# A hybrid mixer trunk: new step costs for the planner that interleaves the instruction streams, and mixer steps ordered behind the dense matmuls on TensorE

## The chip, the cores and the metric

The kernel runs on one core of one Trainium2 chip. The metric is the device time of one execution in microseconds (us); of several runs the median is given. Engines are named as the profile names them: PE is TensorE (PEld its weight loads), DVE VectorE, ACT ScalarE, POOL GpSimd, and SP the engine that issues the DMAs here.

## The reference

One layer, 1024 frames of width 1024, float32. The input is normed and projected by one matrix; three groups of heads (mLSTM, retention, RWKV-7) work on the columns of the result; what they give is projected back; a gated feed-forward follows.

```python
h = rmsnorm(x, ln1_g[l])
p = h @ w_in[l]
pm, pr, pw = jnp.split(p, [M_COLS, M_COLS + R_COLS], axis=-1)
ym = mlstm_group(pm, ...)          # 4 heads, chunkwise state
yr = retention_group(pr)           # 6 heads, chunkwise state
yw = rwkv7_group(pw, ...)          # 6 heads, generalised delta rule
x = x + jnp.concatenate([ym, yr, yw], axis=-1) @ w_out[l]
h = rmsnorm(x, ln2_g[l])
x = x + (jax.nn.silu(h @ w_gate[l]) * (h @ w_up[l])) @ w_down[l]
return rmsnorm(x, lnf_g)
```

In RWKV-7 each frame changes a 64x64 state S per head: `S = S * w - (S kk) (kk a)^T + v k^T`. That is the part that can't be done all at once.

## The kernel before

**The work.** Every float32 operand of a large product is split into a high and a low part (`split_hi` on ACT, line 90; `split_lo` on DVE, line 93), and each product is three matmuls: high by high, high by low, low by high. Two kinds of these are called *dense* here:

- the products by columns in `three` (lines 119 to 121): 128 weights columns by 512 frames, 24 matmuls for a tile, given out in four quarters of 6. They make the 15 channel-major tiles of the in-projection for two halves of 512 frames, and the out-projection.
- the products by frames in `tok_proj` (lines 729 to 731): 128 frames by 256 columns (264 in the first group), 24 matmuls for a tile, given out in two halves of 12.

All other matmuls of the first stage belong to the *mixers*: small ones (64 to 512 columns) between which DVE, ACT, POOL and DMAs work.

**RWKV-7.** The 6 heads are 3 pairs, the frames 2 halves of 8 chunks of 64 frames; so there are 6 pieces (pair i, half h). For each piece:

1. `rwkv_prep` / `rwkv_half` begins with two matmuls (lines 385 and 387), and ends its larger part with 16 Gram matmuls (line 460) whose masked results stand in the tile `E`.
2. `rwkv_inverse` inverts 32x32 triangles: blocks of E go by DMA to DRAM (line 497) and come back to all partitions (line 507), DVE runs a loop of 15 rounds (lines 519 and 522), the result goes to DRAM (line 528) and back into E (line 532), DVE transposes it (line 535), and two rounds of small matmuls (lines 540 and 546) finish it.
3. `rwkv_chain_pair` runs 8 chunks one after the other, each in three steps: matmuls at line 581, an ACT copy `pm` (line 583); matmuls at lines 586 and 590, ACT copies into X (lines 592 and 593); matmuls at lines 597 and 600, a DVE update of X (line 607), with which the next chunk begins. There are 48 chunks in all. The preparation of a piece of the next pair waits for the chain of the same half of this pair, and the chain of a piece waits for its inverse.

mLSTM and retention are 8 chunks each of `attention`.

**The order of the work.** All of these, nine in number, are generators. `weave` runs them against a planner's clock: a step `yield cost, delay` moves the clock by its cost on PE, and makes the generator ready again after the delay; `yield "name"` waits for a `signal`. Of the ready generators the first in the list goes on: the chain, the inverse, the preparation, the output of RWKV, the norms, the attention, and then the three that hold the dense work (`sharing`). So the numbers in the yields decide between which dense matmuls each mixer step is written down. They are worth nothing on the chip itself; there only the order counts. The framework's compile-time scheduler takes the order in which the kernel is written down as the priority, and may still move an instruction ahead of others of its engine where it thinks these are not ready. On the chip PE takes its matmuls in the compiled order.

After the weave come the out-projection of the second half of frames (with the splits of the first operands of the feed-forward beside it) and the feed-forward (lines 1200 to 1202 and 1385 to 1387). The change does not touch these.

Of the kernel before, what the change touches and what calls it, by code (L numbers as in the profile page):

```python
# [23 lines left out]
KT = 8  # L24
# [30 lines left out]
def trunk_kernel(ctx: ExitStack, tc: tile.TileContext, a: dict, out: bass.AP):  # L55
    nc = tc.nc
    V, S, G, PE, SY = nc.vector, nc.scalar, nc.gpsimd, nc.tensor, nc.sync
# [58 lines left out]
    def three(ps, w, xh, xl, ks=range(KT)):  # L116
        for k in ks:
            hi, lo = w[k]
            PE.matmul(ps, lhsT=hi, rhs=xh[:, k, :], start=(k == 0), stop=False)  # L119
            PE.matmul(ps, lhsT=hi, rhs=xl[:, k, :], start=False, stop=False)  # L120
            PE.matmul(ps, lhsT=lo, rhs=xh[:, k, :], start=False, stop=(k == KT - 1))  # L121

    clock, events = [0.0], {}

# [3 lines left out]
    def weave(gens, sharing):  # L131
        live = [[0.0, None, g] for g in gens + sharing]
        holder = None
        while live:
            ready = [math.inf if (holder and s is not holder and s[2] in sharing) else
                     max(s[0], events.get(s[1], math.inf)) if s[1] else s[0] for s in live]
            clock[0] = max(clock[0], min(ready))
            s = next(s for s, r in zip(live, ready) if r <= clock[0])
            got = next(s[2], None)
            if s is holder:  # L140
                holder = None
            if got is None:
                live.remove(s)
            elif isinstance(got, str):
                s[0], s[1] = clock[0], got
            else:
                clock[0] += got[0]
                s[0], s[1] = clock[0] + got[1], None
                if len(got) == 3:
                    holder = s  # L150

    QUARTERS = (range(0, 2), range(2, 4), range(4, 6), range(6, 8))
    PART = 6 * 0.214

# [34 lines left out]
    NT = 9  # L189
    LAT = 0.93  # L190
    CHAIN, INV, ATT, NORM, MIX = 3.51, 20.16, 3.09, 3.26, 1.28

# [14 lines left out]
    xh, xl = zip(*([act.tile([P, KT, HF], F32R, name="act", tag="act") for _ in two] for _ in two))  # L207
# [86 lines left out]
    w = first[2][0]  # L294
# [86 lines left out]
    def rwkv_half(i, h, r, k, v):  # L381
# [17 lines left out]
        G.tensor_tensor(rn, rn, neghalf[:, 0:8], ALU.pow)  # L399
        yield 0.9, 3.0  # L400

# [29 lines left out]
        if h:  # L431
            signal(f"taken{i}", 3.0)
        yield 2.6, 5.0
        pe = misc_tile()
        for t in range(4):
            for q in range(2):
                PE.matmul(pe[rows_of(q), t * P:(t + 1) * P],
                          lhsT=rn[:, 2 * t + q:2 * t + q + 1].broadcast_to([P, 64]), rhs=ident,
                          start=True, stop=True)
# [8 lines left out]
        for q in range(2):  # L448
# [4 lines left out]
            G.tensor_tensor(E[rows, :, q, 192:256], c3(r)[rows], er[rows, :, 1:65], ALU.mult)  # L453
        yield 0.9, 5.5
        for c0 in range(0, 8, 4):
# [18 lines left out]
        signal(f"ab{i}{h}", 3.0)  # L474
        yield 3.4, 3.0
        V.tensor_tensor(kb, kb, er[:, :, 64:65].unsqueeze(3).broadcast_to([P, 8, 2, 64]), ALU.mult)
# [7 lines left out]
        signal(f"prep{i}{h}", 1.0)  # L484
        yield 0.9, 1.0

# [13 lines left out]
    def rwkv_inverse():  # L500
        for i in range(3):
            for h in range(2):
# [5 lines left out]
                for g in range(4):  # L508
                    S.copy(out=R[lane(g)], in_=MN[lane(g), g::4, :])
                yield 0.0, 8.0  # L510

# [4 lines left out]
                for u in range(1, 31, 2):  # L516
                    n, w = (u + 4) // 4, 31 - u
# [12 lines left out]
                for q in range(2):  # L530
                    for b in range(2):
                        SY.dma_start(out=E[blk(q, b), :, q, col(b)], in_=r_d[b, q].rearrange("c s t -> s c t"))
                yield 0.0, 7.5
                for q in range(2):
# [15 lines left out]
                signal(f"inv{i}{h}", 2.5)  # L550
                yield 0.9, 3.0

# [4 lines left out]
    def rwkv_chain_pair(i):  # L557
        st = None
        for h in range(2):
# [3 lines left out]
            for c in range(8):  # L563
# [19 lines left out]
                S.copy(out=pm, in_=chn[:, 0:64])  # L583
                yield 0.2, LAT
                for q in range(2):
# [7 lines left out]
                S.copy(out=X[64:128, c, 1, :], in_=chn[64:128, 64:128])  # L593
                yield 0.2, LAT
                for q in range(2):
# [19 lines left out]
                if c % 4 == 3:  # L615
                    norm_factor(yw, var, 4, 64e-5)
                    signal(f"yw{len(yws)}", 8.0)
                    yws.append(yw)
                yield 0.4, CHAIN
            signal(f"chain{i}{h}", 1.0)  # L620
# [3 lines left out]
    def rwkv_out():  # L624


        yield "gate"
        for i in range(3):
            for h in range(2):
                yield f"prep{i}{h}"  # L630
                for b in range(2):
                    n = 4 * i + 2 * h + b
                    sl = slice(b * 256, b * 256 + 256)
                    gate = lambda: sb.tile([P, 256], F32, name="gate", tag="gate", bufs=2)
                    add, ga = gate(), gate()
                    SY.dma_start(out=add, in_=add_dram[h][i][:, sl])
                    SY.dma_start(out=ga, in_=gate_dram[h][3 + i][:, sl])
                    G.tensor_tensor(add, add, ga, ALU.mult)
                    gl = gate()
                    SY.dma_start(out=gl, in_=gate_dram[h][i][:, sl])  # L640
                    yield f"yw{n}"
                    if i == 2:
                        yield f"proj{h}"
                    yw = yws[n]
                    pt = misc_tile()[:, 0:256]
                    for c in range(4):
                        for q in range(2):
                            o = rows_of(1 - q)
                            PE.matmul(pt[rows_of(q), c * 64:(c + 1) * 64], lhsT=yw[o, c, :], rhs=ident[o, o], start=True, stop=True)
                    signal(f"out{n}", 0.5)  # L650
                    V.tensor_tensor(gl, gl, pt, ALU.mult)
                    V.tensor_tensor(gl, gl, add, ALU.add)
                    if i < 2:
                        SY.dma_start(out=yw_dram[h][i][:, sl], in_=gl)
                    else:
                        yh, yl = yT[h]
                        split_hi(yh[:, 7, sl], gl)
                        split_lo(yl[:, 7, sl], gl, yh[:, 7, sl])
                    yield 0.9, 0.0

# [46 lines left out]
    def tok_proj(g, ts=range(KT)):  # L707
# [16 lines left out]
        for t in ts:  # L724
# [3 lines left out]
            for k in range(KT):  # L728
                PE.matmul(o, lhsT=xh[h][:, k, sl], rhs=w[k][0], start=(k == 0), stop=False)  # L729
                PE.matmul(o, lhsT=xh[h][:, k, sl], rhs=w[k][1], start=False, stop=False)  # L730
                PE.matmul(o, lhsT=xl[h][:, k, sl], rhs=w[k][0], start=False, stop=(k == KT - 1))  # L731
                if k == 3:
                    yield 12 * 0.42e-3 * n, 0.0, True
            vt = etmp(256, "vt")
# [25 lines left out]
            SY.dma_start(out=v_dram[h][sl, 256 * g:256 * g + 256], in_=vt)  # L760
            cost = 12 * 0.42e-3 * n
            yield (cost, 0.0, True) if t < ts.stop - 1 else (cost, 0.0)
# [335 lines left out]
    def attention():  # L1098
        mlstm = ("mlstm", 2.6, mlstm_load, mlstm_chunk, mlstm_finish, None)
        ret = ("ret", 4.0, ret_load, ret_chunk, ret_finish, ret_store)  # L1100
        for (name, cost, load, chunk, finish, store), start, ts in (
# [437 lines left out]
```

## Time and profile before

| | before |
|---|---|
| median of 3 runs | 1536.41 us (1533.66 to 1537.58) |
| the profiled execution | 1537.23 us, of which the profile's span is 1535.4 us |
| PE busy, share of the span | 1425.2 us, 93% |
| DVE / ACT / POOL busy | 883.0 / 556.7 / 453.3 us |
| first matmul of the feed-forward (line 1200) | at 807.0 us |
| DMA | 165.59 MB, mean 108 GB/s |

The profile shows one execution. PE's busy time counts a matmul from its start until its end, and neighbours overlap; so a busy PE is not a PE at its peak, and what a matmul costs is read from the distance between starts. A wait is put down to the instruction that came last before it ended. "PEclk" is the clock granted to TensorE, as a share of full speed.

### The profile page before, as it was taken

The numbers are of one execution on the slowest core, as the hardware profiler recorded it, in microseconds if no ns is written. First come the engines' busy times: TensorE is split into PE (matmuls) and PEld (weight loads), VectorE is DVE, ScalarE is ACT, GpSimd is POOL, SyncE is SP. The second block draws the span as 40 slices with busy tenths as digits, with TensorE's granted clock in tenths as the row PEclk, the third lists the DMA queues.
The fourth block names the chain that finished last, engine by engine and source line by source line (L and its number), as shares of the span: only waits on it lengthen the run. The fifth ranks groups of instructions, "written<-read, shape, count | busy, mean of one in ns | idle before, by whom it ended". The sixth has DMA issues, their size and how long they took to land. (4 is left out here: it accounts for less than half of the span.)

```text
span 1535.4 us, 23068 instructions
## 1 busy us (share of the span) xinstructions
PE 1425.2 (93%) x8434; PEld 1154.8 (75%) x8434; DVE 883.0 (58%) x1750; ACT 556.7 (36%) x1201; POOL 453.3 (30%) x550
## 2 busy tenths in 40 slices
PE   7988899799997998999997999999999998999996
PEld 5767577787677877887785777777777776887886
DVE  7457567458856767545566544555554555337344
ACT  6343244333332143244554333333332344324222
POOL 3211013234434323324336443444444420000000
PEclk9998799899988999799999999999999999999999
DMA  5132121333421343453632222212222248336333
GB/s 210 50 128 71 40 80 68 86 96 104 122 78 52 95 149 109 123 159 121 218 125 68 76 82 83 74 66 80 83 76 77 75 171 283 98 93 226 109 94 117
DMA packets 122334, 165.59 MB, mean 108 GB/s; under 512 B 37837, under 2 KB 70509, under 8 KB 120941
## 3 DMA queue, kind: packets, MB, share of 16 engines
q1 hardware_dynamic: 122220, 164.13, 33.5%
q8 instruction: 66, 1.08, 0.3%
q14 instruction: 48, 0.39, 0.1%
HBM read 125.27 MB, written 38.81 MB: 107 GB/s over the span
## 5 line engine op out<-in xcount | busy, mean ns | idle before, releaser
L93 DVE TENSOR_TENSOR wlo<-wraw,whi 128x512 fp32r<-128x512 f32 (+1 forms) x210 | 147.0, 705 | 131.0 <-ACT whi L90 130.0
L90 ACT ACTIVATE whi<-wraw 128x512 fp32r<-128x512 f32 (+1 forms) x210 | 127.7, 612 | 209.1 <-PE chain L1386 119.8
L93 DVE TENSOR_TENSOR wlo<-rg,whi 128x512 fp32r<-128x512 f32 x128 | 97.9, 767 | 136.2 <-ACT whi L90 136.1
L729 PE MATMUL acc<-whi,act 128*128 128x256 f32 (+1 forms) x512 | 160.8, 317 | 5.9 <-ACT whi L90 4.8
L730 PE MATMUL acc<-wlo,act 128*128 128x256 f32 (+1 forms) x512 | 154.7, 304 | 3.7 <-DVE wlo L93 3.5
L119 PE MATMUL acc<-act,whi 128*128 128x512 f32 x352 | 151.0, 429 | 6.8 <-ACT whi L90 6.1
L1200 PE MATMUL acc<-act,whi 128*128 128x512 f32 x352 | 141.1, 401 | 15.1 <-ACT work L1303 10.7
L731 PE MATMUL acc<-whi,act 128*128 128x256 f32 (+1 forms) x512 | 152.4, 299 | 0.0
L1385 PE MATMUL chain<-act,whi 128*128 128x512 f32 (+1 forms) x374 | 142.9, 382 | 3.9 <-ACT act L90 3.9
L120 PE MATMUL acc<-act,whi 128*128 128x512 f32 x352 | 144.5, 411 | 1.8 <-DVE act L252 1.8
L121 PE MATMUL acc<-act,wlo 128*128 128x512 f32 x352 | 144.9, 412 | 1.1 <-DVE wlo L93 1.1
L90 ACT ACTIVATE whi<-rg 128x512 fp32r<-128x512 f32 x128 | 79.1, 628 | 178.5 <-PE acc L1201 81.1
L1386 PE MATMUL chain<-act,whi 128*128 128x512 f32 (+1 forms) x374 | 143.0, 383 | 0.8 <-DVE act L93 0.8
L1387 PE MATMUL chain<-act,wlo 128*128 128x512 f32 (+1 forms) x374 | 142.7, 382 | 0.0
L1202 PE MATMUL acc<-act,wlo 128*128 128x512 f32 x352 | 139.3, 396 | 0.2 <-DVE wlo L93 0.2
L1201 PE MATMUL acc<-act,whi 128*128 128x512 f32 x352 | 139.1, 395 | 0.0
L729 PEld LDWEIGHTS acc<-whi,act 128*128 128x128 f32 x512 | 103.8, 204 | 13.6 <-ACT whi L90 5.3
L730 PEld LDWEIGHTS acc<-wlo,act 128*128 128x128 f32 x512 | 104.4, 204 | 8.1 <-DVE wlo L93 5.6
L1200 PE MATMUL misc<-act,whi 128*128 128x512 f32 x264 | 104.6, 396 | 4.7 <-ACT whi L90 4.7
L731 PEld LDWEIGHTS acc<-whi,act 128*128 128x128 f32 x512 | 104.5, 204 | 1.1 <-issue 0.2
L1201 PE MATMUL misc<-act,whi 128*128 128x512 f32 x264 | 104.6, 396 | 0.0
L1202 PE MATMUL misc<-act,wlo 128*128 128x512 f32 x264 | 104.2, 395 | 0.0
(323 smaller groups left out, 2832.3 us busy)
## 6 DMA issues: line engine op xcount, KB each, us to landing
wraw<-in_w_down SPq DMA_DIRECT2D x85, 256.0 KB, 2.7
rg<-in_w_gate SPq DMA_DIRECT2D x22, 512.0 KB, 5.6
rg<-in_w_up SPq DMA_DIRECT2D x22, 512.0 KB, 5.0
a_dram<-work SPq DMA_DIRECT2D x43, 256.0 KB, 2.2
wraw<-in_w_tm SPq DMA_DIRECT2D x40, 256.0 KB, 3.0
rg<-a_dram SPq DMA_DIRECT2D x10, 1024.0 KB, 6.3
v_dram<-vt SPq DMA_DIRECT2D x64, 128.0 KB, 1.9
wraw<-in_w_out SPq DMA_DIRECT2D x32, 256.0 KB, 3.4
```

What stands on the lines that cost most here:

```text
L90: S.activation(hi, src, AF.Copy, scale=scale)
L93: (eng or V).tensor_tensor(lo, src, hi.bitcast(F32), ALU.subtract)
L119: PE.matmul(ps, lhsT=hi, rhs=xh[:, k, :], start=(k == 0), stop=False)
L120: PE.matmul(ps, lhsT=hi, rhs=xl[:, k, :], start=False, stop=False)
L121: PE.matmul(ps, lhsT=lo, rhs=xh[:, k, :], start=False, stop=(k == KT - 1))
L729: PE.matmul(o, lhsT=xh[h][:, k, sl], rhs=w[k][0], start=(k == 0), stop=False)
L730: PE.matmul(o, lhsT=xh[h][:, k, sl], rhs=w[k][1], start=False, stop=False)
L731: PE.matmul(o, lhsT=xl[h][:, k, sl], rhs=w[k][0], start=False, stop=(k == KT - 1))
L1200: PE.matmul(ps, lhsT=hi, rhs=hi_x[:, k, :], start=(start and k == 0), stop=False, skip_group_check=True)
L1201: PE.matmul(ps, lhsT=hi, rhs=lo_x[:, k, :], start=False, stop=False, skip_group_check=True)
L1202: PE.matmul(ps, lhsT=lo, rhs=hi_x[:, k, :], start=False, stop=(stop and k == 3), skip_group_check=True)
L1386: PE.matmul(ps, lhsT=hi, rhs=lo_a[:, sl], start=False, stop=False)
```

## The change

Three things are done, all in the weave of the first stage:

1. The planner's numbers are others. The dense work costs 7 to 12% more (`PART`, a quarter, 6 * 0.214 to 6 * 0.23; a token half from 12 * 0.42e-3 to 12 * 0.47e-3 for each column). The steps of the mixers cost and delay much more: the chain's three steps go from (0.2, 0.93), (0.2, 0.93), (0.4, 3.51) to (0.4, 1.4), (0.45, 1.9), (0.5, 4.2), the loop of the inverse from 20.16 to 30.0, its trips through DRAM from 8.0 and 7.5 to 11.0 and 9.0, an mLSTM chunk from 2.6 to 4.2, a retention chunk from 4.0 to 5.0. The two costs of the output of RWKV and of one step of the preparation become smaller.
2. The planner's clock begins at 10 and not at 0.
3. Every mixer step is traced within `tc.issue_after(dense[0])`, where `dense[0]` is the last dense matmul written down so far (the third of each k). It gives each PE instruction of the step an ordering edge to that matmul: the compile-time scheduler may no longer put it ahead of that matmul. No semaphore is added, since both run on PE. A dense matmul may still be put ahead of a mixer step, and the other engines' instructions get no edge.

No instruction is added or removed. The lines of the changed kernel below line 122 have numbers that are 2 higher.

```diff
@@ three
-            PE.matmul(ps, lhsT=lo, rhs=xh[:, k, :], start=False, stop=(k == KT - 1))
+            dense[0] = PE.matmul(ps, lhsT=lo, rhs=xh[:, k, :], start=False, stop=(k == KT - 1)).ins
...
-    clock, events = [0.0], {}
+    clock, events = [10.0], {}
+    dense = [None]
@@ weave
-            got = next(s[2], None)
+            with nullcontext() if s[2] in sharing or dense[0] is None else tc.issue_after(dense[0]):
+                got = next(s[2], None)
...
-    PART = 6 * 0.214
+    PART, TOK = 6 * 0.23, 12 * 0.47e-3
...
-    LAT = 0.93
-    CHAIN, INV, ATT, NORM, MIX = 3.51, 20.16, 3.09, 3.26, 1.28
+    LAT, CHAIN, INV, ATT, NORM, MIX = (1.4, 1.9), 4.2, 30.0, 4.0, 4.0, 1.6
@@ tok_proj
-                PE.matmul(o, lhsT=xl[h][:, k, sl], rhs=w[k][0], start=False, stop=(k == KT - 1))
+                dense[0] = PE.matmul(o, lhsT=xl[h][:, k, sl], rhs=w[k][0], start=False, stop=(k == KT - 1)).ins
```

Two places show how this moves the instructions on PE. A name left of the arrow is the tile written, those right of it are read; `acc` is the result of dense work, `whi` and `wlo` are split weights, `act` split activations, `chain` the chain's tile, `misc` that of the other mixers.

The first is PE in the third chunk of the first pair. Before, from the chain's first step (L581) to its second (L586, L590):

```order
L581 MATMUL chain<-X,E 64x64 x2
L119 MATMUL acc<-act,whi 128x512
L120 MATMUL acc<-act,whi 128x512
L121 MATMUL acc<-act,wlo 128x512
L119 MATMUL acc<-act,whi 128x512
L120 MATMUL acc<-act,whi 128x512
L121 MATMUL acc<-act,wlo 128x512
L586 MATMUL chain<-pm,E 64x64 x2
L590 MATMUL chain<-st,E 64x64 x2
```

Now, from the same first step (L583):

```order
L583 MATMUL chain<-X,E 64x64 x2
L119 MATMUL acc<-act,whi 128x512
L120 MATMUL acc<-act,whi 128x512
L121 MATMUL acc<-act,wlo 128x512
L119 MATMUL acc<-act,whi 128x512
L120 MATMUL acc<-act,whi 128x512
L121 MATMUL acc<-act,wlo 128x512
L119 MATMUL acc<-act,whi 128x512
L120 MATMUL acc<-act,whi 128x512
L121 MATMUL acc<-act,wlo 128x512
L119 MATMUL acc<-act,whi 128x512
L120 MATMUL acc<-act,whi 128x512
```

One more dense matmul and then the second step follow: 12 stand between the two steps where 6 stood.

The second is PE ahead of the last of the six inverses, where its first round of small matmuls begins (L540, now L542, reading `tq`). Before, with chunks of the retention (L952 to L975) and frame products of the in-projection (L729 to L731) in front of it:

```order
L952 MATMUL misc<-rT 128x128 x6
L962 MATMUL misc<-RR,rT 128x64 x3
L729 MATMUL acc<-whi,act 128x256
L730 MATMUL acc<-wlo,act 128x256
L966 MATMUL misc<-rv,rsw 128x64 x3
L962 MATMUL misc<-RR,rT 128x64 x3
L731 MATMUL acc<-whi,act 128x256
L729 MATMUL acc<-whi,act 128x256
L975 MATMUL misc<-rv,rk 64x64 x6
L730 MATMUL acc<-wlo,act 128x256
L966 MATMUL misc<-rv,rsw 128x64 x3
L540 MATMUL misc<-tq,E 32x32
```

Now, with the chain (L583 to L602) and products of the out-projection (L119 to L121):

```order
L588 MATMUL chain<-pm,E 64x64 x2
L592 MATMUL chain<-st,E 64x64 x2
L120 MATMUL acc<-act,whi 128x512
L121 MATMUL acc<-act,wlo 128x512
L599 MATMUL chain<-X,E 64x64 x2
L602 MATMUL chain<-X,E 64x64 x2
L998 MATMUL misc<-cst,ry 128x128 x3
L119 MATMUL acc<-act,whi 128x512
L583 MATMUL chain<-X,E 64x64
L120 MATMUL acc<-act,whi 128x512
L121 MATMUL acc<-act,wlo 128x512
L542 MATMUL misc<-tq,E 32x32
```

The whole in-projection stands ahead of this place now; the chain's steps follow each other with one to three dense matmuls between them.

More of the change, by code (lines that the diff above doesn't have):

```diff
@@ L1 @@
 import math
-from contextlib import ExitStack
+from contextlib import ExitStack, nullcontext
 from itertools import chain
@@ L399, in rwkv_half @@
         G.tensor_tensor(rn, rn, neghalf[:, 0:8], ALU.pow)
-        yield 0.9, 3.0
+        yield 2.6, 4.0
         S.activation(t1, th, AF.Identity, scale=hka[:, i:i + 1], bias=oka[:, i:i + 1])
@@ L432, in rwkv_half @@
             signal(f"taken{i}", 3.0)
-        yield 2.6, 5.0
+        yield 2.0, 6.0
         pe = misc_tile()
@@ L453, in rwkv_half @@
             G.tensor_tensor(E[rows, :, q, 192:256], c3(r)[rows], er[rows, :, 1:65], ALU.mult)
-        yield 0.9, 5.5
+        yield 1.2, 7.0
         for c0 in range(0, 8, 4):
@@ L474, in rwkv_half @@
         signal(f"ab{i}{h}", 3.0)
-        yield 3.4, 3.0
+        yield 2.2, 4.0
         V.tensor_tensor(kb, kb, er[:, :, 64:65].unsqueeze(3).broadcast_to([P, 8, 2, 64]), ALU.mult)
@@ L484, in rwkv_half @@
         signal(f"prep{i}{h}", 1.0)
-        yield 0.9, 1.0
+        yield 1.0, 1.0
     blk = lambda q, b: slice((1 - q) * 64 + b * 32, (1 - q) * 64 + b * 32 + 32)
@@ L509, in rwkv_inverse @@
                     S.copy(out=R[lane(g)], in_=MN[lane(g), g::4, :])
-                yield 0.0, 8.0
+                yield 0.0, 11.0
                 mf = MN.rearrange("p s t -> p (s t)")
@@ L532, in rwkv_inverse @@
                         SY.dma_start(out=E[blk(q, b), :, q, col(b)], in_=r_d[b, q].rearrange("c s t -> s c t"))
-                yield 0.0, 7.5
+                yield 0.0, 9.0
                 for q in range(2):
@@ L550, in rwkv_inverse @@
                 signal(f"inv{i}{h}", 2.5)
-                yield 0.9, 3.0
+                yield 1.7, 3.0
     def rwkv_chain():
@@ L583, in rwkv_chain_pair @@
                 S.copy(out=pm, in_=chn[:, 0:64])
-                yield 0.2, LAT
+                yield 0.4, LAT[0]
                 for q in range(2):
@@ L593, in rwkv_chain_pair @@
                 S.copy(out=X[64:128, c, 1, :], in_=chn[64:128, 64:128])
-                yield 0.2, LAT
+                yield 0.45, LAT[1]
                 for q in range(2):
@@ L618, in rwkv_chain_pair @@
                     yws.append(yw)
-                yield 0.4, CHAIN
+                yield 0.5, CHAIN
             signal(f"chain{i}{h}", 1.0)
@@ L658, in rwkv_out @@
                         split_lo(yl[:, 7, sl], gl, yh[:, 7, sl])
-                    yield 0.9, 0.0
+                    yield 0.7, 0.0
     def rwkv_gate():
@@ L730, in tok_proj @@
                 PE.matmul(o, lhsT=xh[h][:, k, sl], rhs=w[k][1], start=False, stop=False)
-                PE.matmul(o, lhsT=xl[h][:, k, sl], rhs=w[k][0], start=False, stop=(k == KT - 1))
+                dense[0] = PE.matmul(o, lhsT=xl[h][:, k, sl], rhs=w[k][0], start=False, stop=(k == KT - 1)).ins
                 if k == 3:
-                    yield 12 * 0.42e-3 * n, 0.0, True
+                    yield TOK * n, 0.0, True
             vt = etmp(256, "vt")
@@ L760, in tok_proj @@
             SY.dma_start(out=v_dram[h][sl, 256 * g:256 * g + 256], in_=vt)
-            cost = 12 * 0.42e-3 * n
+            cost = TOK * n
             yield (cost, 0.0, True) if t < ts.stop - 1 else (cost, 0.0)
@@ L1098, in attention @@
     def attention():
-        mlstm = ("mlstm", 2.6, mlstm_load, mlstm_chunk, mlstm_finish, None)
-        ret = ("ret", 4.0, ret_load, ret_chunk, ret_finish, ret_store)
+        mlstm = ("mlstm", 4.2, mlstm_load, mlstm_chunk, mlstm_finish, None)
+        ret = ("ret", 5.0, ret_load, ret_chunk, ret_finish, ret_store)
         for (name, cost, load, chunk, finish, store), start, ts in (
```

## The prediction

> **What bounds the kernel now.** I read the page first, then the stretches by stage, PE's timeline, PE's waits, and then the stretches around each inverse.
>
> ```profile
> span 1535.4 us, 23068 instructions
> ...
> PEclk9998799899988999799999999999999999999999
> ```
>
> ```profile
> 0.00:171.00 171.00, 143.63 (x788) 111.49 (x788) 101.73 (x206) 75.89 (x140) 34.32 (x60) 0.92 0.33 108
> 171.00:807.00 636.00, 591.80 (x4628) 487.80 (x4628) 409.74 (x1022) 241.13 (x664) 214.78 (x349) 0.93 0.36 109
> 807.00:1535.40 728.40, 689.75 (x3020) 555.55 (x3018) 371.56 (x523) 239.70 (x397) 204.21 (x142) 0.99 0.32 107
> ```
>
> The first row gives the clock granted to PE in 40 slices: the dips lie in the first half. In the stretches the columns are time, then busy time of PE, PEld, DVE, ACT, POOL, then that clock. The feed-forward from 807 us on has PE busy for 690 of 728 us at a clock of 0.99, and the change doesn't touch it. The first 807 us are where PE has gaps (592 of 636 us) and a clock of 0.92 to 0.93. Busy time hides how much is lost there, so I go by the distance between starts:
>
> ```profile
> 184.74 0.34 PE L581 MATMUL chain<-X,E 128*64 128x64 f32 x4
> 185.80 0.39 PE L119 MATMUL acc<-act,whi 128*128 128x512 f32 x1
> 186.03 0.40 PE L120 MATMUL acc<-act,whi 128*128 128x512 f32 x1
> ...
> 193.28 0.34 PE L581 MATMUL chain<-X,E 128*64 128x64 f32 x4
> 318.15 0.28 PE L731 MATMUL acc<-whi,act 128*128 128x256 f32 x1
> 318.27 0.28 PE L729 MATMUL acc<-whi,act 128*128 128x256 f32 x1
> ```
>
> A dense matmul of 512 columns costs 0.23 us, one of 256 costs 0.12 us, at full clock. These are the new planner's numbers (PART is 6 x 0.23; TOK at 256 columns is 12 x 0.12). In this piece nothing is lost: a chunk of the chain takes 193.28 - 184.74 = 8.54 us and holds 30 dense matmuls (6.9 us) and 10 mixer matmuls, which leaves 0.16 us for each mixer matmul. Where it is lost, the waits say:
>
> ```profile
> PE misc L540 <- DVE tq L535: 10.7, 3, 7.5
> PE chain L586 <- ACT pm L583: 7.6, 5, 1.9
> PE chain L597 <- ACT X L593: 6.7, 3, 5.3
> PE misc L460 <- DVE E L468: 4.9, 4, 3.1
> PE acc L729 <- ACT whi L90: 4.8, 2, 4.4
> PE chain L581 <- DVE X L607: 4.7, 1, 4.7
> ```
>
> The inverse and the chain lead: PE comes to a mixer step before its operand is there, and everything behind it in the queue stands. How much that is with the lower clock it brings, I take from the five stretches from the last Gram matmul of a piece (L460) to the first matmul that needs its inverse (L540), pieces 2 to 6:
>
> ```profile
> L460 PE MATMUL misc<-E,kb x32: 272/272/419, 129.8 to 137.3; 64*128 64x128 f32 x32
> L540 PE MATMUL misc<-tq,E x32: 191/191/212, 215.4 to 215.9; 32*32 32x32 f32 x32
> L460 PE MATMUL misc<-E,kb x32: 272/272/373, 272.3 to 277.6; 64*128 64x128 f32 x32
> L540 PE MATMUL misc<-tq,E x32: 191/191/212, 331.7 to 332.2; 32*32 32x32 f32 x32
> L460 PE MATMUL misc<-E,kb x32: 272/272/373, 371.4 to 375.2; 64*128 64x128 f32 x32
> L540 PE MATMUL misc<-tq,E x32: 191/191/212, 428.5 to 431.2; 32*32 32x32 f32 x32
> L460 PE MATMUL misc<-E,kb x32: 272/272/550, 465.7 to 473.9; 64*128 64x128 f32 x32
> L540 PE MATMUL misc<-tq,E x32: 191/236/258, 529.5 to 533.0; 32*32 32x32 f32 x32
> L460 PE MATMUL misc<-E,kb x32: 272/272/373, 573.1 to 577.3; 64*128 64x128 f32 x32
> L540 PE MATMUL misc<-tq,E x32: 236/236/257, 642.2 to 645.9; 32*32 32x32 f32 x32
> ```
>
> In the stretches between those places (the same columns as above):
>
> ```profile
> 137.30:215.40 78.10, 70.59 (x417) 50.85 (x416) 43.85 (x116) 21.78 (x61) 8.83 (x32) 0.83 0.21 55
> 277.60:331.70 54.10, 44.82 (x367) 40.26 (x365) 28.94 (x95) 14.51 (x54) 13.32 (x29) 0.87 0.32 87
> 375.20:428.50 53.30, 49.98 (x371) 36.99 (x369) 43.24 (x143) 20.67 (x63) 22.45 (x48) 1.00 0.41 108
> 473.90:529.50 55.60, 49.67 (x408) 45.20 (x407) 37.25 (x113) 12.13 (x43) 17.90 (x32) 0.88 0.25 72
> 577.30:642.20 64.90, 56.26 (x488) 50.56 (x487) 43.15 (x127) 20.91 (x60) 21.82 (x33) 0.86 0.32 96
> ```
>
> **The inverse windows.** Between those two places the compiled order has, before: 207 dense matmuls of 512 columns and 108 mixer matmuls; 235 of 256 and 71; 108 of 512 and 138; 289 of 256 and 62; 211 of 256 and 155. At 0.23, 0.12 and 0.15 us (a mixer matmul: an estimate, just under the chain's 0.16, since many others are as small) that is PE work of 63.8, 38.9, 45.5, 44.0 and 48.6 us. They took 78.1, 54.1, 53.3, 55.6 and 64.9 us. So 14.3, 15.2, 7.8, 11.6 and 16.3 us were lost, 65 us in all, at a clock of 0.83 to 0.88 in all but the third.
>
> After: 283 of 512 and 86; 275 of 256 and 156; 132 of 512, 97 of 256 and 58; 249 of 256 and 159; 57 of 512 and 154. That is 78.0, 56.4, 50.7, 53.8 and 36.2 us of PE work. The total work is the same, so what counts is what is lost. The shortest inverse took 53.3 us, and the first four windows now hold about that or more; so PE arrives when the result is there. I take 3 us lost in each (bounds: 0, as in the chunk above, and what each lost before), 12 instead of 48.9: **-37 us**. The sixth piece is the reverse: 36.2 us of work for an inverse of 53.3 to 64.9 us. I take 56, near the three shorter ones, since with fewer dense products DVE has fewer evictions in its queue: 20 lost instead of 16.3, **+4 us** (bounds 17 and 29: +1 and +12).
>
> [...]
>
> **The chain.** Of its waits (7.6 + 6.7 + 4.7 = 19 us) I put half inside the windows above. Of the other half I take **-5 us** (bounds 0 and -9.5): between its steps stand 12 dense matmuls instead of 6 early on, which is 2.8 us against 1.4. Late on they stand tighter. In the last ten chunks seven have about 3.3 us of PE work in all three steps. One of the quickest chunks in the trace:
>
> ```profile
> 376.55 0.34 PE L581 MATMUL chain<-X,E 128*64 128x64 f32 x4
> ...
> 377.48 0.33 PE L586 MATMUL chain<-pm,E 64*64 64x64 f32 x4
> ...
> 378.98 0.34 PE L597 MATMUL chain<-X,E 128*64 128x64 f32 x4
> ```
>
> 0.93 and 1.50 us, though some dense work stood between them; the third step, which has a DVE update behind it and not one ACT copy, I estimate at 2 us, a third more than the second. That makes 4.4 us, 1.1 over the work, times seven: **+8 us** (bounds 0, if the waits overlap other mixers' work, and 8.54 - 3.3 = 5.2 a chunk, +37).
>
> **The rest.** The preparations (from L385 to the last L460) hold about as much PE work after as before in the order; I take nothing for them, and nothing for the clock's start at 10, since the order up to the first inverse is the same but for 26 dense matmuls. DMA issues move with their steps, and SP's queue is taken in order too:
>
> ```profile
> SPq L101 <- DVE R L522: 34.7, 10, 17.7
> ```
>
> Weight loads (L101) stood behind the issue of an inverse's result (L528), which waited for its DVE loop, for up to 17.7 us. The loop counts 30 instead of 20 now, so that issue is written down later, behind more weight loads. That can only help dense work; I take nothing, since PE's own waits for weights are the few above. DVE and ACT see the same instructions; more dense work inside a window also means more evictions and splits in front of the inverse's loop, which is the second rival.
>
> **The edge.** A mixer step behind a dense matmul now waits where that matmul waits for its split weights (4.8 us above, once 4.4). I take nothing, since the order puts the step there on purpose and the weights are loaded ahead. [...] Were that wait doubled by it, the sum would be 5 us worse.
>
> Sum: -37 + 4 - 5 + 8 = -30 us. Against the profiled execution of 1537.2 us that is 1507 us; the median of the runs lies 0.8 us lower, so **1506 us**.
>
> **The rivals.**
>
> 1. *All of it goes* (0.20). If the windows lose nothing (first four -49, sixth +1), the chain's waits outside go (-9.5), and the preparations, with the clock no longer halved beside them, give 10 (an estimate from the 0.07 of clock that 171 to 807 us lacks, 45 us if all of it were matmul time, less what the windows hold): -68, 1469 us. For it: where PE is fed, a chunk loses nothing. Against: the waits at L460 are not paced anew.
> 2. *DVE sets the pace* (0.10). The inverse is mostly a DVE loop, and DVE takes its queue in order: 43.2 of 53.3 us and 43.2 of 64.9 us busy in the third and fifth rows. If a window with more dense work has a longer loop for the evictions in it, the first four lose what they lost, and -5 + 4 + 0 to 8 remain: 1536 to 1544, about 1538 us.
> 3. *The cover runs out, slower* (0.13). Dense work is spent early (12 between steps), and the last inverse and the chain behind it stand bare. Its price: -37 - 5, the sixth inverse at 64.9 (+12), seven chunks at 8.54 us (+37): +7, 1544 us. It decides from about 7.5 us for a bare chunk: (37 + 5 - 12) / 7 = 4.3 over 3.3. Against: those 8.54 us contain 6.9 us of dense work that isn't there.
> 4. *The change does not do what it says.* The compiled order excludes that for the numbers. The edge alone may do nothing; the forecast rests on the order, whichever made it.
>
> **How the numbers follow.** The forecast has 0.52 (its own range is 1488 to 1523 us: from 1.5 us lost in a window, the sixth at +1, the chain at -7 and no tail, to 6 us lost in a window, the chain at -2 and the tail at +8), rival 1 0.20, rival 2 0.10, rival 3 0.13; 0.05 lies between. A measurement of this kernel can tell about 0.3%, 4.6 us. Faster: forecast, rival 1 and the 0.05 in between, 0.77. Same: most of rival 2, 0.09. Slower: rival 3 and the rest of rival 2, 0.14. The range takes in rival 1 nearly and rival 2: 1470 to 1540 us.
>
> **What would show it.** Right: the first matmul of the feed-forward at about 777 us instead of 807; the wait at the inverse's matmuls (now L542) concentrated in the sixth piece, 15 to 25 us in one; a granted clock near 1.0 in the stretches of pieces 2 to 5; the chain's early chunks at 12 to 13 us each (48 dense matmuls at 0.23 and 10 others at 0.16 us) and yet no gap on PE. Wrong: a clock still under 0.9 in those stretches, or loops of the inverse that grew with the work beside them (rival 2); chain steps late on over 7 us a chunk (rival 3).

## The result, and the profile after

The change made the kernel slower, by 0.6%: 1543.35 us, the median of 13 runs (1539.38 to 1552.2), beside 1535.65 us, the median of 13 runs of the kernel before on the same chip. The ratio is 1.0059, its 95% interval 1.0039 to 1.0080. Forecast were 1506 us, and 1470 to 1540 us as the range; the time lies outside it. Here and below medians are of all runs, while ratios leave out the few that took over 1.5% longer than the fastest of their kernel (one of the kernel before here, two of chain_first_pair).

The profiled execution took 1540.95 us, 1539.2 us of it span. First the clock granted to PE in 40 slices, then the three stages (time; busy time of PE, PEld, DVE, ACT, POOL; clock), as shown of before:

```profile
PEclk9999998989899989998998999999999999999998
```

```profile
0.00:171.00 171.00, 148.37 (x815) 115.59 (x816) 104.66 (x213) 77.81 (x143) 35.75 (x63) 0.95 0.32 109
171.00:806.40 635.40, 585.07 (x4602) 482.51 (x4602) 397.32 (x1016) 238.45 (x661) 213.04 (x346) 0.92 0.36 109
806.40:1539.20 732.80, 695.99 (x3019) 560.32 (x3017) 369.67 (x524) 240.27 (x398) 205.82 (x142) 0.98 0.32 106
```

The feed-forward, which should have begun at 777 us, begins at 806.4 us, where it began before (807 us), and the clock from 171 us on is 0.92, where it was 0.93. The weave has gained nothing in this execution. How much of the 8 us of the medians lies in it can't be read from one pair of profiles: the runs before_again and after_again, below, show that two executions of one kernel differ by more.

The same five stretches as before, from the last Gram matmul of pieces 2 to 6 (now L462) to the first matmul that needs the piece's inverse (now L542):

```profile
138.70:223.10 84.40, 80.23 (x450) 60.84 (x448) 56.60 (x133) 27.36 (x64) 9.29 (x34) 0.94 0.22 64
308.40:383.80 75.40, 67.26 (x573) 60.04 (x571) 52.02 (x179) 19.35 (x67) 32.32 (x59) 0.90 0.41 108
425.00:484.10 59.10, 52.67 (x340) 42.13 (x339) 39.83 (x116) 14.81 (x43) 19.90 (x34) 0.94 0.29 81
531.20:599.80 68.60, 63.23 (x534) 57.14 (x533) 45.26 (x133) 23.19 (x68) 21.06 (x37) 0.88 0.40 115
648.80:705.40 56.60, 43.37 (x331) 32.98 (x330) 31.53 (x103) 15.32 (x51) 20.62 (x31) 0.89 0.35 102
```

More work does stand in the first four (450 matmuls where there were 417, then 573 for 367, 340 for 371, 534 for 408; the third of these pairs, of the fourth piece, has fewer but larger ones), and together they became longer by just about that work: 46 us for 47.5. To see what each loses, I took from the trace the distance from each matmul's start to the next, and compared it with 0.23 us for a dense matmul of 512 columns, 0.12 us for one of 256, and the median distance of its own line for a mixer matmul. What is over that is lost (us; "again" is a second execution of the same kernel):

| window of piece | before: length, work, lost | before again: lost | after: length, work, lost | after again: lost |
|---|---|---|---|---|
| 2 | 78.1, 57.0, 21.1 | 16.1 | 84.4, 72.0, 12.4 | 13.5 |
| 3 | 54.1, 36.6, 17.5 | 18.3 | 75.4, 56.3, 19.2 | 19.6 |
| 4 | 53.3, 45.0, 8.3 | 8.6 | 59.1, 48.1, 11.0 | 11.9 |
| 5 | 55.6, 41.4, 14.2 | 12.8 | 68.5, 51.1, 17.4 | 16.5 |
| 2 to 5 | 61.1 | 55.8 | 60.0 | 61.5 |
| 6 | 64.9, 44.6, 20.3 | 20.9 | 56.6, 33.8, 22.8 | 23.6 |

Windows 2 to 5 lose 60 us, where 12 were forecast. Only the second loses less than before, in both executions. And hardly any of it is a wait for the inverse. PE's waits over the whole weave, after:

```profile
PE misc L542 <- DVE tq L537: 13.1, 3, 9.6
PE chain L588 <- ACT pm L585: 10.2, 4, 6.4
```

Of the 13.1 us at the inverse's matmul, 9.6 stand ahead of the sixth inverse and the rest at the first (158 to 162 us, inside the second window); in the windows of pieces 3, 4 and 5 PE waits for no inverse at all. In the fourth this is the only wait that the profile gives:

```profile
PE chain L588 <- ACT pm L585: 6.4, 1, 6.4
```

PE at that place, and then ACT:

```profile
437.97 0.34 PE L583 MATMUL chain<-X,E 128*64 128x64 f32 x4
...
439.63 0.28 PE L733 MATMUL acc<-whi,act 128*128 128x256 f32 x1
446.34 0.48 PE L588 MATMUL chain<-pm,E 64*64 64x64 f32 x4 [6.43 <-ACT pm L585]
...
446.96 0.79 PE L119 MATMUL acc<-act,whi 128*128 128x512 f32 x1
447.55 0.63 PE L120 MATMUL acc<-act,whi 128*128 128x512 f32 x1
```

```profile
434.90 0.21 ACT L612 COPY yw<-chain 128x64 f32<-128x64 f32 x1 [2.09 <-DVE X L609]
443.03 1.66 ACT L511 COPY R<-MN 32x256 f32<-32x256 f32 x4 [7.92 <-DMA MN<-ab_d]
444.71 0.22 ACT L613 ACTIVATE ysq<-chain 128x64 f32<-128x64 f32 x1
...
446.10 0.19 ACT L585 COPY pm<-chain 128x64 f32<-128x64 f32 x1
```

The chain's first step was issued at 437.97 us. Its ACT copy `pm` could follow at once, but ACT stands from 435 to 443 us at the inverse's R copies (L511), whose operand MN is still on its way by DMA. `pm` comes at 446.10 us, behind these copies, a statistic and two splits, and PE, with its next dense matmuls queued behind the chain's second step, stands 6.4 us and then runs 512 columns in 0.43 to 0.59 us instead of 0.23, at a granted clock of 0.50 (446.9 to 449.8 us). Over the whole of this execution ACT and DVE start their instructions in the compiled order, line by line (1201 and 1750 instructions; the same in before), and here `pm` comes behind a copy that stood 7.92 us. No planner's number moves the R copies: they are written down right behind the issue of the DMA, ahead of the step's `yield`.

### The profile page after: what moved, and what is told of

The parts are those of the page before. It is cut to its first block, busy times and chain, and to the rows that moved or that the text cites. A ratio compares the mean times of both kernels' runs of the same rounds, so it can differ in the third digit from the quotient of the medians.

```text
span 1539.2 us, 23089 instructions
## 1 busy us (share of the span) xinstructions
PE 1429.4 (93%) x8434; PEld 1158.4 (75%) x8434; DVE 871.6 (57%) x1750; ACT 556.5 (36%) x1201; POOL 454.6 (30%) x550
## 5 line engine op out<-in xcount | busy, mean ns | idle before, releaser
L731 PE MATMUL acc<-whi,act 128*128 128x256 f32 (+1 forms) x512 | 156.6, 308 | 4.6 <-ACT whi L90 3.8
L119 PE MATMUL acc<-act,whi 128*128 128x512 f32 x352 | 149.9, 426 | 6.5 <-ACT whi L90 6.1
L733 PE MATMUL acc<-whi,act 128*128 128x256 f32 (+1 forms) x512 | 151.6, 296 | 0.0
L121 PE MATMUL acc<-act,wlo 128*128 128x512 f32 x352 | 143.9, 409 | 2.1 <-DVE wlo L93 2.1
L731 PEld LDWEIGHTS acc<-whi,act 128*128 128x128 f32 x512 | 101.5, 199 | 11.6 <-ACT whi L90 4.8
L733 PEld LDWEIGHTS acc<-whi,act 128*128 128x128 f32 x512 | 102.5, 200 | 2.5 <-issue 1.7
```

The costliest lines, as they stand in the source:

```text
L733: dense[0] = PE.matmul(o, lhsT=xl[h][:, k, sl], rhs=w[k][0], start=False, stop=(k == KT - 1)).ins
```

## The experiments

Two explanations stood after the profiles: that the windows lose because ACT and DVE stand in their queues for the inverse's transfers (theory Q), whatever the numbers say; and that the new numbers move dense work away from where it is needed (S, later split by part of the table). Rivals were the edge, and the inverse's loop. Ratios are to runs of the kernel before on the same chip; intervals are 95%. "After" and "before" name the kernels on which an edit is made. The letters of the theories are those of the expectations: E the edge, Q the queues that stand at a DMA's landing, D DVE's loop as the pace, S dense work spent too early, O the other numbers as the cost, L the later chain steps.

### numbers_only and edge_only: the two halves of the change

numbers_only is after without the edge:

```diff
-            with nullcontext() if s[2] in sharing or dense[0] is None else tc.issue_after(dense[0]):
-                got = next(s[2], None)
+            got = next(s[2], None)
```

> The new planner numbers without the ordering edge. Theory Q (what PE loses comes from ACT and DVE standing in their queues for DMA landings of the inverse): the edge matters little, within 4 us of the changed kernel (1539 to 1547). Theory E (the edge ate the gain: mixer steps held behind late dense matmuls): 10 to 30 us faster than the changed kernel, 1515 to 1533.

edge_only is before with those lines added, and its old numbers.

> The kernel before with the ordering edge alone. Theory Q: within 4 us of before. Theory E: 5 us or more slower than before.

Measured: 1539.8 us, 1.0033 [1.0005, 1.0061], and 1533.21 us, 0.9987 [0.9968, 1.0006]. The edge by itself can't be told from nothing, and the numbers without it are slower as the whole change is. So the cost lies in the numbers; what the edge does beside them (1.0033 against 1.0059) is within the noise.

### after_r_dma: ACT out of the inverse's transfer

```diff
                 for g in range(4):
-                    S.copy(out=R[lane(g)], in_=MN[lane(g), g::4, :])
+                    SY.dma_start(out=R[lane(g)], in_=ab_d.rearrange("b q c s t -> (b q c) s t")[:, g::4, :])
```

> The changed kernel, but the four ACT copies of R from MN are four DMAs from the same DRAM tile, so ACT no longer stands in its queue until MN has landed. Theory Q: the stalls of PE that end with a chain or attention step just after MN lands (2.6, 3.2, 6.7, 3.0 and 3.6 us in the changed kernel's trace) go, with some of the half-clock time behind them: 12 to 25 us faster than the changed kernel, 1518 to 1531. Theory D (the DVE loop of the inverse sets the length of the windows): no more than 4 us off, 1539 to 1547.

Measured: 1551.12 us, 1.0109 [1.0074, 1.0144], no faster than after (1.0059 [1.0039, 1.0080]), where theory Q had named 12 to 25 us less. Two of PE's waits in the weave:

```profile
PE acc L121 <- DVE wlo L93: 5.6, 2, 5.3
...
PE chain L588 <- ACT pm L585: 3.4, 2, 3.2
```

ACT no longer waits for MN, and PE's wait for `pm` went from 10.2 to 3.4 us as it should. But dense matmuls now wait for `wlo` from DVE, at 445 us 5.3 us in one, close to the place of the 6.4 us of after. DVE there:

```profile
448.37 0.66 DVE L516 TENSOR_TENSOR rt<-MN 128x480 f32<-128x480 f32 x1 [7.66 <-DMA MN<-ab_d]
...
450.67 1.82 DVE L93 TENSOR_TENSOR wlo<-wraw,whi 128x512 fp32r<-128x512 f32 x2
```

DVE too has an instruction in its queue that needs MN, and the evictions and splits behind it wait for 7.7 us. The stall went from one engine's queue to the other's, and MN, whose load is issued 4.8 us later here (438.1 instead of 433.4 us), comes at 448.4 instead of 443.0 us. To take ACT alone out of the way gains nothing; the held kernels below take both.

### after_no_loop: the inverse without its loop

```diff
-                for u in range(1, 31, 2):
+                for u in range(0):
```

> The changed kernel without the 15 rounds of the inverse's DVE loop (the inverse is not computed). Theory D: each inverse is 18 to 33 us shorter, the windows fall to their PE work, some 49 us lost in windows 2 to 5 and 20 in the sixth go: 40 to 65 us faster, 1478 to 1503. Theory Q: the waits at MN stay and only the sixth's wait goes: 8 to 20 us faster, 1523 to 1535.

Measured: 1521.89 us, 0.9921 [0.9899, 0.9942]. Windows 3 and 4, where after has 75.4 and 59.1 us:

```profile
307.60:384.30 76.70, 69.32 (x571) 61.82 (x570) 43.16 (x133) 19.23 (x67) 31.34 (x59) 0.87 0.42 113
422.30:480.80 58.50, 51.92 (x337) 41.46 (x335) 30.83 (x69) 15.80 (x46) 17.88 (x36) 0.94 0.28 82
```

With 9 us of DVE work taken out of each (52.02 and 39.83 against 43.16 and 30.83 us) these windows are as long as in after. The loop doesn't set them. What the kernel gains, some 21 us by the ratios, lies for the most part where PE does wait for the inverse: in the sixth window, which lasts 47.3 instead of 56.6 us, and in the first two (53.0 and 77.1 instead of 58.4 and 84.4 us). The fifth is shorter as well, 62.8 instead of 68.5 us, though PE waits for no inverse there in after; 1.5 us of that is less work between its ends, and the rest isn't explained. Theory D had named 40 to 65 us. By the size of the gain and by windows 3 and 4 it falls, and with it the mechanism of the prediction's second rival.

### chain_numbers and other_numbers: the numbers in two parts

chain_numbers is before with the new numbers of the chain's three steps alone:

```diff
-    CHAIN, INV, ATT, NORM, MIX = 3.51, 20.16, 3.09, 3.26, 1.28
+    LAT, CHAIN, INV, ATT, NORM, MIX = (1.4, 1.9), 4.2, 20.16, 3.09, 3.26, 1.28
...
-                yield 0.2, LAT
+                yield 0.4, LAT[0]
...
-                yield 0.2, LAT
+                yield 0.45, LAT[1]
...
-                yield 0.4, CHAIN
+                yield 0.5, CHAIN
```

> The kernel before with the new numbers of the chain's three steps alone. Theory S (dense work is a fixed amount of cover; slower chain numbers spend it early, and what the chain no longer waits for, attention, the output and the sixth inverse wait for): as slow as the changed kernel or slower, 1540 to 1550. Theory O (it is the other numbers that cost): like before, 1530 to 1539.

other_numbers has all the new numbers but these, and no edge.

> The new numbers without the edge, but with the chain's three steps as before. Theory S: the inverse and the attention get their cover and the chain keeps ahead, 1520 to 1534, faster than before by up to 15 us. Theory O: as slow as the changed kernel, 1540 or more.

Measured: 1576.8 us, 1.0279 [1.0261, 1.0296], and 1518.83 us, 0.9901 [0.9873, 0.9929]. Both go the way of theory S, and further than it said. The change is made of two parts that work against each other: the numbers of the inverse, the attention and the rest gain 15 us, those of the chain cost 43 us by themselves and, on top of the others (1.0033 against 0.9901), about 20. In chain_numbers PE's waits for inverses lead, and one is the longest of the study:

```profile
725.27 0.79 PE L580 MATMUL chain<-X,E 128*64 128x64 f32 x4 [3.17 <-DVE X L606]
746.21 0.31 PE L539 MATMUL misc<-tq,E 32*32 32x32 f32 x2 [20.14 <-DVE tq L534]
```

PE stands for 20 us ahead of the sixth inverse, with 74 us of dense matmuls queued behind that place.

### after_held and before_held: ACT and DVE kept from standing at the transfer

The R copies and DVE's first product on MN are written down 16 of the planner's us after the transfer's issue, where the copies came at once and the product after 11 (or 8, in before), and held by an order edge behind the last ACT copy or split, and the last DVE eviction, split or update of X, that was written down ahead of them (`recent` is set at these):

```diff
-                for g in range(4):
-                    S.copy(out=R[lane(g)], in_=MN[lane(g), g::4, :])
-                yield 0.0, 11.0
+                yield 0.0, 16.0
+                with tc.issue_after(recent["S"]):
+                    for g in range(4):
+                        S.copy(out=R[lane(g)], in_=MN[lane(g), g::4, :])
...
+                with tc.issue_after(recent["V"]):
                     V.tensor_tensor(tv, mf[:, 34:34 + 15 * 66:66].unsqueeze(2).broadcast_to([P, 15, 32]), MN[:, 2:31:2], ALU.mult)
```

> The changed kernel with the inverse's ACT copies and first DVE product written 16 planner us after the load of MN instead of 0 and 11, and held behind the last chain copy, split or eviction written ahead on their engine. Theory Q (ACT and DVE standing in their queues for MN stall PE): the waits of ACT on MN fall from 39 us to under 15, PE's waits on pm copies from 10 us to under 4; 8 to 20 us faster than the changed kernel, 1523 to 1535. Theory S: the waits go elsewhere, and the inverse comes a chunk later: 1540 to 1550.

> The same on the kernel before (16 planner us after the load of MN instead of 0 and 8). Theory Q: 5 to 15 us faster than before, 1520 to 1530. Theory S: 1533 to 1542.

Measured: 1526.9 us, 0.9954 [0.9934, 0.9975], for after, and 1524.31 us, 0.9939 [0.9918, 0.9960], for before: 16 us off the one and 9 off the other. ACT's wait for MN in after's weave, and then in after_held's:

```profile
ACT R L511 <- DMA MN<-ab_d: 39.2, 6, 10.1
```

```profile
ACT R L515 <- DMA MN<-ab_d: 4.1, 2, 3.3
```

At the place of the 6.4 us stall ACT now takes `pm` first, then waits for a weight, and does the R copies without a wait for MN:

```profile
432.19 0.21 ACT L589 COPY pm<-chain 128x64 f32<-128x64 f32 x1 [1.74 <-PE chain L587]
438.47 0.63 ACT L92 ACTIVATE whi<-wraw 128x512 fp32r<-128x512 f32 x1 [6.07 <-DMA wraw<-in_w_cm]
...
439.45 1.66 ACT L515 COPY R<-MN 32x256 f32<-32x256 f32 x4
```

PE's wait for `pm` goes from 10.2 to 2.9 us, and windows 2 to 5 of after_held lose 46.7 us by the same account, where after loses 60.0. The two waits and both times came out as theory Q had said. This part of the loss isn't the change's own: before has it as well (29.1 us of ACT's time at MN, 2.6 in before_held). With the holding, the two kernels can't be told apart (0.9954 and 0.9939), so the 8 us between after and before may lie in such stalls too; that wasn't shown. Nor does a run separate the holding edges from the later place in the order: the edit also moves the rest of the inverse back by 5 (or 8) of the planner's us.

### other_held and other_held_edge: what helps, together

other_held is other_numbers with the same holding; other_held_edge adds the edge.

> The new numbers of all steps but the chain's three, with the R copies and the first VectorE product of each inverse held back behind the last chain work written ahead of them; no edge. Theory Q plus S (the shift of cover and the queues on the inverse's transfer are two separate losses): the gain of the numbers alone (14.5 us) and of the holding (9 to 16 us) add up, 1503 to 1510 us, ScalarE's wait for MN under 8 us in all. Rival O' (both gains come from the same stalls of TensorE, so only one can be had): 1515 to 1520 us. Rival: the holding makes ScalarE late for the gates, no better than the numbers alone or worse, 1519 to 1525 us.

> The kernel of the run other_held with the edge of the change added. Theory E0 (the edge changes nothing, since the scheduler already places the mixers' instructions behind that matmul): within 4 us of other_held. Rival E (the edge keeps ScalarE and VectorE from taking up mixer work early): 5 us or more away from it, in either direction.

Measured: 1506.43 us, 0.9814 [0.9779, 0.9850], and 1499.44 us, 0.9776 [0.9737, 0.9816]. The gains of the numbers and of the holding add up (0.9901 times 0.9939 is 0.984). Between the two kernels lie 7 us, more than the 4 expected, but their intervals overlap: whether the edge helps here stays open. Both are faster than before, by about 2%, and so than after.

### before_again and after_again: how far two executions differ

No edit.

> The kernel before, unchanged, to see how far two profiled executions of one kernel differ. Expected: the first FFN matmul within 3 us of 807.2 us, and 726 to 733 us from there to the end of the span. If the FFN's start lies over 5 us away, differences of some us between profiles say nothing.

> The changed kernel, unchanged, for the same purpose. Expected: the first FFN matmul within 3 us of 806.4 us, and 726 to 733 us from there to the end; windows from the last Gram matmul to the first inverse matmul within 1 us of 58.4, 84.4, 75.4, 59.1, 68.5 and 56.6 us. If the FFN's start comes at 809 or later, the slower time of the change lies in the weave; if at 806, in what differs from run to run behind it.

The stage up to the feed-forward, of before_again and of after_again:

```profile
0.00:794.80 794.80, 721.39 (x5417) 590.44 (x5418) 509.75 (x1228) 316.74 (x805) 249.33 (x409) 0.94 0.36 111
```

```profile
0.00:820.30 820.30, 741.27 (x5416) 605.76 (x5417) 502.65 (x1228) 316.38 (x804) 248.42 (x409) 0.92 0.35 107
```

The feed-forward begins at 794.8 us instead of 807.2, and at 820.3 instead of 806.4. I had expected both within 3 us. So a difference of some 10 us between two profiles of this kernel says nothing, and verdicts must rest on the ratios. The lengths of the windows are steadier (after_again: 58.7, 85.5, 75.9, 60.0, 67.6, 57.5 us, each within about 1 us of after's), and so is the feed-forward itself (730.3 and 731.8 us).

### chain_first_pair and chain_later_pairs: where the chain's numbers cost

other_numbers, with the chain's new numbers in the first of its three pairs, or in the second and third:

```diff
+            steps = ((0.4, 1.4), (0.45, 1.9), (0.5, 4.2)) if i == 0 else ((0.2, LAT[0]), (0.2, LAT[1]), (0.4, CHAIN))
...
-                yield 0.2, LAT[0]
+                yield steps[0]
```

(and so for the other two steps; the counterpart has `if i > 0`).

> The new numbers of all steps but the chain's, no edge, and the chain's new numbers in the first of its three pairs alone (16 of 48 chunks). With the old chain numbers everywhere this took 0.9901 of the time before, with the new ones everywhere 1.0033. Theory S (the dense work spent between the early chain steps is what is missed later): most of the 20 us come with the first pair, 1529 to 1540 us (0.997 to 1.004). Rival L (the later chain steps themselves, written down later and tighter, cost it): 1515 to 1524 us (0.988 to 0.993). If both halves cost about the same, 1525 to 1530 us.

> The counterpart: the chain's old numbers in the first pair, the new ones in the second and third (32 of 48 chunks). Theory S: little cost, 1515 to 1524 us (0.988 to 0.993), since the dense work is still there when the second pair begins. Rival L: 1529 to 1540 us (0.997 to 1.004).

Measured: 1522.16 us, 0.9922 [0.9890, 0.9954], and 1535.51 us, 1.0016 [0.9986, 1.0046]. In the first pair, where 12 dense matmuls now stand between two steps, the new numbers cost nothing that can be told; in the later pairs they cost most of the 20 us. Theory S in this form, that dense work spent early is missed later, falls; the outcome is that of rival L, whose mechanism these two runs don't show. The window of the sixth piece, in chain_first_pair and then in chain_later_pairs:

```profile
618.00:675.60 57.60, 52.66 (x463) 43.30 (x462) 39.03 (x117) 21.64 (x68) 20.01 (x35) 0.94 0.43 128
```

```profile
603.60:684.10 80.50, 70.74 (x557) 60.94 (x555) 44.86 (x129) 24.68 (x71) 19.00 (x35) 0.81 0.39 112
```

By the account used above they lose 15.4 us at a clock of 0.94, and 28.4 us at 0.81. In the second, PE's longest wait, 6.8 us, again begins with ACT at the inverse's transfer: the first `vt` of ACT stands behind it, POOL and DVE need that `vt`, and ACT's second `vt` waits for them. PE and ACT:

```profile
621.04 0.28 PE L731 MATMUL acc<-whi,act 128*128 128x256 f32 x1
628.16 1.23 PE L954 MATMUL misc<-rT 64*128 64x128 f32 x8 [6.84 <-ACT rT L946]
```

```profile
622.16 1.66 ACT L510 COPY R<-MN 32x256 f32<-32x256 f32 x4 [6.16 <-DMA MN<-ab_d]
623.84 0.37 ACT L757 ACTIVATE vt<-acc,rhalf 128x128 f32<-128x128 f32 x1
626.99 0.37 ACT L757 ACTIVATE vt<-acc,rhalf 128x128 f32<-128x128 f32 x1 [2.78 <-DVE vt L753]
627.26 0.85 ACT L946 COPY rT<-misc 128x384 f32<-128x384 f32 x2
```

Over the kernels the sixth window loses 18.5 us in other_numbers, 15.4 with the chain's new numbers in the first pair, 28.4 with them in the later pairs, 24.5 with them everywhere and 30.6 in chain_numbers. That is 6 of the 20 us for the new numbers everywhere, and 10 of the 18 us for those in the later pairs. The rest is spread over stretches in which single profiles differ by as much, and where it goes wasn't shown.

## Why the prediction was wrong, point by point

**The step that failed** is the main term, 3 us lost in each of windows 2 to 5, where 60 us were lost in the four: "so PE arrives when the result is there. I take 3 us lost in each", -37 us. Its first half came true: with more work in the windows, PE has no wait for the inverse in pieces 3 to 5. Its second half doesn't follow, since the loss in those windows had, for the most part, not been a wait for the inverse either. Before, the waits that the profile gives in the fifth window are these two:

```profile
PE acc L729 <- ACT whi L90: 4.4, 1, 4.4
PE misc L540 <- DVE tq L535: 1.4, 1, 1.4
```

The wait of 7.5 us, the longest of the row that the prediction quotes ("10.7, 3, 7.5"), lies ahead of the first inverse, which is still running when the second window begins:

```profile
154.08 0.40 PE L119 MATMUL acc<-act,whi 128*128 128x512 f32 x1
161.99 0.28 PE L540 MATMUL misc<-tq,E 32*32 32x32 f32 x2 [7.51 <-DVE tq L535]
```

In windows 2 to 4 the profile gives no wait for the window's own inverse. So of the 61 us that windows 2 to 5 lost before, 1.4 us was PE waiting for that. All waits there together are 25.7 us, the 7.5 us at the first inverse among them and the others mainly for `pm`, X and `whi` of ACT and X of DVE; the remaining 35 us are the lower clock (0.83, 0.87 and 0.88 in windows 2, 3 and 5; 1.00 in window 4) and matmuls over their best distance. In the second, which held the long wait for an inverse, the loss fell (21.1 and 16.1 us before, 12.4 and 13.5 after). In the other three the added work brought losses along: together they lose 48 us after in both executions, where they lost 40. The row quoted in the prediction already held a bound: of 10.7 us in all at the inverse, 8.9 lay in these windows, and the gain of 37 took their whole loss for such waits and what they bring. Nor did the signs that the prediction named come: the clock in the four windows is 0.94, 0.90, 0.94 and 0.88, not near 1.0, and the feed-forward began 29 us later than it said.

**A term put at nothing.** For what lies between the five windows, the preparations above all, the prediction took nothing, since the work there is about the same. The stretch from the second inverse to the last Gram matmul of the third piece, before and after:

```profile
215.40:277.60 62.20, 60.00 (x479) 45.72 (x476) 48.07 (x94) 29.76 (x77) 17.92 (x35) 1.00 0.24 79
```

```profile
223.10:308.40 85.30, 76.88 (x675) 66.77 (x671) 42.07 (x99) 32.28 (x95) 24.43 (x45) 0.92 0.27 85
```

By the account above it holds 10 us more work, and it loses 19.0 us where it lost 6.4; the second executions lose 22.6 and 6.6. That is the largest rise of any stretch of the weave, and about as much as the windows of the first two pieces gain (7.1 and 8.7 us in the first pair of executions, 5.8 and 2.6 in the second). The longest wait in it, 3.5 us, is at the gates of mLSTM (L828, for ACT's `gl`); the rest of the rise isn't explained.

**A slip in the counting.** The work of each window was counted from the compiled order, where one row can stand for several matmuls (x2, x8); I counted rows. So did the 0.16 us of the quoted chunk: its 10 rows are 20 matmuls, of 0.08 us each. The second window was taken as 207 dense and 108 others, 315 in all; the row of the stretch, quoted beside it, says 417. The price of 0.15 us was too high by more than the count was too low, so the work came out 0.5 to 6.8 us too large in each before, and 0.1 to 6 us after. It changed no conclusion: with the right counts the four windows lost 61 us instead of 48.9, and the same step would have forecast still more.

**The sixth window: right in time.** 56.6 us, forecast 56; it loses 22.8 instead of 20.3 us, forecast +4. The reason given, fewer evictions in DVE's queue, was not tested. The wait at the inverse there is one of 9.6 us, below the 15 to 25 us named:

```profile
695.45 0.33 PE L583 MATMUL chain<-X,E 128*64 128x64 f32 x2
705.35 0.31 PE L542 MATMUL misc<-tq,E 32*32 32x32 f32 x2 [9.58 <-DVE tq L537]
```

**The chain: about right in time.** First steps of chunks early and late, after:

```profile
181.35 0.34 PE L583 MATMUL chain<-X,E 128*64 128x64 f32 x4
...
194.10 0.34 PE L583 MATMUL chain<-X,E 128*64 128x64 f32 x4
...
751.01 0.34 PE L583 MATMUL chain<-X,E 128*64 128x64 f32 x4
755.43 0.33 PE L583 MATMUL chain<-X,E 128*64 128x64 f32 x2
...
760.74 0.33 PE L583 MATMUL chain<-X,E 128*64 128x64 f32 x2
```

An early chunk takes 12.75 us (forecast 12 to 13), these late ones 4.4 and 5.3 us (forecast 4.4; over 7 would have been wrong). The short ones among the last ten take up to 6.5 us, most of them with more work than the 3.3 us counted; two that hold 48 and 42 dense matmuls take 12.7 and 11.8 us. The term of +8 us was sized from such chunks against that work; by the account of lost time, though, the stretch from the sixth inverse to the last chain step loses 9.3 us, where it lost 14.0. The term was too careful and its sign is open. Of the chain's waits, -5 us outside the windows was too much: only 4.9 of 19 us lay outside them before (14.1 in windows 3, 4 and 6), and 3.0 lie there after.

**The edge: right**, nothing, as far as a ratio of 0.9987 [0.9968, 1.0006] can tell.

**The rivals.** The time of 1543 us is that of rivals 2 and 3 (1538 and 1544 us), and neither was right for its reason. Rival 2 had the right outcome, windows that lose what they lost, and the wrong mechanism: DVE's loop doesn't pace them (after_no_loop, windows 3 and 4). Rival 3 had the right part of the change, the chain's numbers, and the wrong place: the tail's chunks are not 8.5 us long, and spending dense work early costs nothing (chain_first_pair). What the prediction had no rival for is that the table of numbers could hold a gain of 15 us and a loss of 20, and that the inverse's transfer costs time by standing in the queues of ACT and DVE (7.92 us at one place in after; 16 and 9 us came off with the holding), not by its own length.

**What stays open:** why the chain's numbers cost in the later pairs beyond what the sixth window shows, what makes the stretch after the second inverse lose more, how the 35 us without a wait divide, and whether the edge helps once ACT and DVE are held.

## What to carry to other kernels

Before a gain is booked against a wait, add up that wait's own rows inside the stretch; time lost in a stretch is not time lost to the wait that the stretch is named after. An instruction that needed a DMA's result held what stood behind it on its engine, for 7.92 us on ACT in after and 7.66 us on DVE in after_r_dma. So look where ACT or DVE stand at a landing, and write such an instruction down later; here the edit that did so was worth 9 and 16 us without changing any work. A table of many numbers is tested in parts, since its halves can hide each other.

## What the runs showed of the hardware

A lowered clock behind a wait. In before, PE stood 7.51 us ahead of the first inverse (the row at 161.99 us above), and behind it:

```profile
162.20:176.40 14.20, 14.20 (x105) 9.47 (x104) 7.38 (x26) 3.59 (x12) 1.35 (x4) 0.50 0.06 20
```

Dense matmuls of 512 columns start 0.43 us apart there instead of 0.23. Beside the preparation of the fifth piece, from 443.6 to 451.8 us, the clock of before was 0.50 too.

A lowered clock without a gap. From 366 to 400 us of after, about the end of the third window, PE has one wait, of 0.9 us, and yet:

```profile
368.60:378.80 10.20, 9.29 (x86) 8.29 (x86) 6.18 (x16) 4.02 (x14) 6.35 (x9) 1.00 0.42 103
378.80:399.30 20.50, 20.50 (x157) 15.93 (x157) 7.93 (x25) 8.04 (x18) 8.21 (x13) 0.50 0.49 133
```

For 20.5 us the granted clock was 0.50 while PE was busy for all 20.50 of them. In after_again it is the same at this place, 20.5 us from 385.0 us, with PE busy throughout; in numbers_only it lasts 30.7 us from 381.6 us. PE's one wait, of 0.9 us, lies ahead of this stretch, at a clock of 1.00; what lowered the clock was not tried.
